# A hybrid decoder layer: joint maxima behind the last far scores, earlier splits of the output weights, value halves stored apart

## The chip, the cores and the metric

The kernel runs on one core of a Trainium2 chip. It is one program of some 17,000 instructions on five engines: TensorE (matrix products and transposes, PE in the profile; its weight loads are PEld), VectorE (DVE), ScalarE (ACT), GpSimd (POOL) and SyncE (SP), whose queue issues the DMAs. Each engine works through its own row of instructions in order, and waits at an instruction until the semaphores that it needs have come. The metric is the device time of one execution in microseconds.

## The reference

One decoder layer on 1024 tokens of width 1024:

```python
h = rmsnorm(x, mix_pre_norm)
q_a, k_a, v_a, q_h, f_h, i_h, g_h = split(h @ w_in)
attn = dilated_mixture_attention(q_a, k_a, v_a, slopes)   # 8 heads of 64
attn = rmsnorm(attn, attn_out_norm)
rec = hgrn2_recurrence(q_h, f_h, i_h, g_h, lower_bounds)  # 4 heads of 128
x = x + rmsnorm(concat([attn, rec]) @ w_out, mix_post_norm)
h = rmsnorm(x, mlp_pre_norm)
x = x + rmsnorm(square(relu(h @ w_ff1)) @ w_ff2, mlp_post_norm)
```

In the attention a token sees keys in three dilated windows, and the three softmaxes are joined by their denominators. That is one softmax over all keys with a table of biases. The recurrence ends in `o = rmsnorm(o) * silu(gate)`. All is float32.

## The kernel before

A float32 product is made of three passes: each operand is split into a high part, which TensorE takes in its fast form, and the low rest, and high by high, high by low and low by high are added. Such a split is a copy on ScalarE (`hi`) and a subtraction on VectorE (`lo = src - hi`, L85 and L86). The weights come as tiles of 128 by 1024 in the order of a list, `stream`. `w_load` (L102) fetches the next one into one of two raw buffers, `w_split` (L109) splits the next one and then asks for a further load, and `w_get(i)` (L125) splits all up to `i`. The eight tiles of the output weights follow those of the projections in this list, from WO0 on. `WO_TAG` says in which kind of buffer their parts lie: a pair of names is two slab buffers, None the two buffers `wh` and `wl` of the projections. The profile calls the parts `woh` and `wol` in the first case, `wh` and `wl` in the second.

The four recurrent heads come first (`hgrn_core`, L453), then the eight attention heads, two to a pair. The gate products (`gated`, L608) are the end of a recurrent head: eight VectorE instructions of 128 by 128 that multiply the normed output, still in PSUM, by the gate. For the last recurrent head they are put off into the attention, four in step 0 and four in step 2.

The attention is a hand-written loop of 64 steps (L1244), eight to a head. A step belongs to one piece of the scores of its head: D0 to D3 are the first four blocks of 128 rows, F0 and F1 the far keys of the later rows (by class of four), N0 and N1 their near keys. For a piece there is

- `look` (L813): two score matmuls into a bank of kind "s"; VectorE adds the bias, writes the scores to SBUF and takes the maximum of each row (a custom instruction and a read of its accumulator, L842);
- `raise_` (L881): ScalarE's exponential with the negative maximum as bias;
- `turn` (L894): TensorE transposes the exponentials into a bank of kind "t"; ScalarE copies the high part out, VectorE subtracts the low part;
- `weigh` (L936) and `finish` (L975): the product with the values, and a transpose back.

There are two banks of each kind. A matmul into one waits until what stood in it two banks ago has been read.

The far and the near scores of a row share one maximum, but their rows lie in two orders. So the maxima are carried over: `spread_max` (L862) is a VectorE product of the maxima with a selector, `swap_max` (L870) two small TensorE matmuls into a bank "s" (the profile's `px`), and `joint` (L875) two small VectorE instructions that take the larger maximum and negate it. `joint(hd, 0)` ends the maxima of the far rows and must stand before their exponentials, `joint(hd, 1)` does so for the near rows. Before the change the near maxima are spread at the end of step 0 and swapped at the end of step 1, the far ones spread at the end of step 2 and swapped at the end of step 3; `joint(hd, 0)` opens step 3 and `joint(hd, 1)` step 4 (steps counted within the head).

Between these pieces `fill` (L172) takes matmuls from a queue of generators, so many per step as `UNITS` says: first the projections of the coming pairs (`attn_proj`, L728), from step 47 on the first half of the output product (`early_out`, L1092, TensorE's `pwe`), for which rows of the recurrence's result are multiplied by a gain on GpSimd (`row_rec`, L1033, the profile's `erows`) and transposed (`row_turn`, L1066, `pmt` and `emt`). What is to be done at a certain step beside that stands in a table, `hooks` (L1214). Steps 40 to 47 are head 5, 48 to 55 head 6, 56 to 63 head 7. `drain` (L187) issues all that is left in the queue.

The values of a pair are made in two halves of 512 tokens. `values_turn` (L712) transposes a half (`pvt`, from VectorE's `vf`), splits it, and after the second half stores both to DRAM with four DMAs. `far_load` (L637) loads the values of the far keys from there in another order with six DMAs, into two tiles. `key_job` (L695) copies a piece of the keys' high part, subtracts the low part on GpSimd (`kl`), and lets SyncE copy both to the other half of the partitions.

## Time and profile before

| | us |
|---|---|
| median of 3 runs | 1214.13 (1213.41 to 1214.55) |
| the profiled execution | 1214.51 |
| its span, first to last instruction | 1212.7 |
| TensorE busy | 1198.3 (99%) |
| VectorE busy | 868.8 (72%) |
| ScalarE busy | 546.6 (45%) |
| GpSimd busy | 326.3 (27%) |
| TensorE between 450 and 500 us | 46.09 of 50 |

The granted TensorE clock was 0.999. The profile divides the span into forty slices; TensorE is at nine tenths or more in all but the first and the last. The end of a matmul is modelled, so two neighbours overlap in the listing, and a wait shows as a late start with the idle time in brackets and the instruction that ended it. The attention's 64 steps run from 306 to about 520 us; step 40 begins near 443 and step 47 near 466. A step is found in TensorE's row by its transposes: one to four for D0 to D3, three for F0 and F1, four for N0 and N1.

### The profile page before, as it was taken

To read this page: it belongs to the slowest core of one execution; us is meant where nothing else is said; L and a number is where in the kernel's file an instruction comes from. 1 tells how busy PE (TensorE), PEld (TensorE's weight loads), DVE (VectorE), ACT (ScalarE), POOL (GpSimd) and SP (SyncE) were. 2 spreads that over 40 slices of the span, in tenths; PEclk is the share of its full clock that TensorE was granted. 3 is DMA by queue.
4 is the path that set the end of the run, shared out by engine and by line. 5 is a ranking of instruction groups with operands and counts; after the bars stand their busy time and mean duration, and the time that the engine had idled before them with its cause. 6 is when DMAs were issued, how large, how long until landed. Compare 5 with 4: busy or idle time off the path is not lost.

```text
span 1212.7 us, 17220 instructions
## 1 busy us (share of the span) xinstructions
PE 1198.3 (99%) x6350; PEld 1026.8 (85%) x6350; DVE 868.8 (72%) x1478; ACT 546.6 (45%) x1067; POOL 326.3 (27%) x321
## 2 busy tenths in 40 slices
PE   8999999999999999999999999999999999999998
PEld 8898989888888887888888888888888888888886
DVE  5697878777666767677689566766678554478796
ACT  7633333322565657755565222222234453534562
POOL 0110102022221213254230886575631000000022
PEclk9999999999999999999999999999999999999999
DMA  5231323123544546364514555553587534433337
GB/s 218 69 94 58 104 75 108 36 82 75 141 109 117 141 118 146 104 218 145 188 64 156 182 174 209 192 185 140 199 324 266 212 92 152 158 102 100 109 104 278
DMA packets 86483, 174.21 MB, mean 144 GB/s; under 512 B 12160, under 2 KB 38784, under 8 KB 86400
## 3 DMA queue, kind: packets, MB, share of 16 engines
q1 hardware_dynamic: 86400, 173.12, 44.0%
q8 instruction: 50, 0.82, 0.3%
q14 instruction: 33, 0.27, 0.1%
HBM read 117.76 MB, written 49.04 MB: 138 GB/s over the span
## 4 chain that ended last, share of the span: by engine, by line
PE 93%; DVE 2%; ACT 2%; DMA 1%; issue 1%; POOL 0%; SPq 0%; DVEq 0%; POOLq 0%; ACTq 0%
PE f L1940 18%; PE f2s L1940 7%; PE pig L91 2%; PE pig L89 2%; PE pig L90 2%; PE pl L480 2%; PE pwo L91 2%; PE pwo L89 2%; PE pwo L90 2%; PE pm_ak L89 1%; PE pm_f L89 1%; PE pm_ak L91 1%; PE pm_ak L90 1%; PE pm_f L91 1%; PE pm_f L90 1%; PE pm_av L89 1%
## 5 line engine op out<-in xcount | busy, mean ns | idle before, releaser
L86 DVE TENSOR_TENSOR al<-ar,ah 128x1024 fp32r<-128x1024 f32 x56 | 70.6, 1261 | 80.7 <-ACT ah L85 80.6
L1940 PE MATMUL f<-bh,ah 128*128 128x512 f32 x320 | 124.5, 389 | 0.0
L1940 PE MATMUL f<-bl,ah 128*128 128x512 f32 x320 | 124.5, 389 | 0.0
L1940 PE MATMUL f<-bh,al 128*128 128x512 f32 x320 | 124.5, 389 | 0.0
L85 ACT ACTIVATE ah<-ar 128x1024 fp32r<-128x1024 f32 x56 | 59.1, 1056 | 87.5 <-DMA ar<-actd 87.2
L1940 PEld LDWEIGHTS f<-bh,al 128*128 128x128 f32 x320 | 60.1, 188 | 12.6
L1940 PEld LDWEIGHTS f<-bl,ah 128*128 128x128 f32 x320 | 60.1, 188 | 12.5
L1940 PEld LDWEIGHTS f<-bh,ah 128*128 128x128 f32 x320 | 60.1, 188 | 12.3
L2014 POOL TENSOR_SCALAR lbl<-ssq 128x1 f32<-128x1 f32 x4 | 3.3, 819 | 245.7 <-ACT fd L2010 245.6
L1563 POOL TENSOR_TENSOR e<-x,e 128x512 f32<-128x512 f32 x14 | 21.6, 1540 | 131.0 <-DVE x L1514 123.8
L1940 PE MATMUL f2s<-bl,ah 128*128 128x512 f32 (+1 forms) x128 | 48.9, 382 | 0.0
L1940 PE MATMUL f2s<-bh,al 128*128 128x512 f32 (+1 forms) x128 | 48.9, 382 | 0.0
L1940 PE MATMUL f2s<-bh,ah 128*128 128x512 f32 (+1 forms) x128 | 48.9, 382 | 0.0
L671 POOL COPY tout<-traw 128x256 f32<-128x256 f32 x16 | 12.2, 763 | 107.9 <-DMA traw<-in_bias_tab_dram 74.2
L991 POOL TENSOR_TENSOR anat<-anat,stat 128x128 f32<-128x128 f32 (+1 forms) x24 | 13.4, 559 | 102.4 <-DVE anat L990 91.1
L86 DVE TENSOR_TENSOR bl<-br,bh 128x1024 fp32r<-128x1024 f32 x32 | 40.1, 1253 | 1.1 <-ACT bh L85 1.0
L1957 ACT ACTIVATE acc<-f 128x512 f32<-128x512 f32 x28 | 16.7, 598 | 49.4 <-PE f L1940 49.4
L86 DVE TENSOR_TENSOR wl<-raw,wh 128x1024 fp32r<-128x1024 f32 x23 | 30.1, 1310 | 10.9 <-ACT wh L85 10.9
L85 ACT ACTIVATE bh<-br 128x1024 fp32r<-128x1024 f32 x32 | 33.6, 1050 | 3.7 <-PE f L1940 2.4
L707 POOL TENSOR_TENSOR kl<-kf,kh 64x512 fp32r<-64x512 f32 x16 | 22.2, 1390 | 39.8 <-ACT kh L706 36.8
L751 POOL TENSOR_TENSOR ql<-qf,q 64x512 fp32r<-64x512 f32 x16 | 21.4, 1340 | 42.4 <-ACT q L750 41.8
L89 PE MATMUL pwo<-woh,mt 128*128 128x512 f32 x80 | 31.6, 395 | 0.0
(1702 smaller groups left out, 4022.5 us busy)
## 6 DMA issues: line engine op xcount, KB each, us to landing
ar<-actd SPq DMA_DIRECT2D x56, 512.0 KB, 3.7
br<-in_w_ff_dram SPq DMA_DIRECT2D x16, 1024.0 KB, 6.3
w1r<-in_w_ff_dram SPq DMA_DIRECT2D x14, 1024.0 KB, 6.5
raw<-in_w_in_dram SPq DMA_DIRECT2D x26, 512.0 KB, 4.0
actd<-e SPq DMA_DIRECT2D x17, 768.0 KB, 4.3
actd<-e SPq DMA_DIRECT2D x11, 1024.0 KB, 4.1
vd<-v SPq DMA_DIRECT2D x16, 256.0 KB, 3.9
raw<-in_w_out_dram SPq DMA_DIRECT2D x8, 512.0 KB, 3.7
```

The lines of the kernel that those rows point to most:

```text
L85: S.activation(hi, src, AF.Copy)
L86: eng.tensor_tensor(out=lo, in0=src, in1=f32(hi), op=ALU.subtract)
L89: TE.matmul(dst, lhs[0], rhs[0], start=start, stop=False)
L90: TE.matmul(dst, lhs[0], rhs[1], start=False, stop=False)
L91: TE.matmul(dst, lhs[1], rhs[0], start=False, stop=stop)
L480: TE.matmul(pl[:, n % 2, :192], kt[:, n * P:(n + 1) * P], sets[u // 2][:, n % 4], start=True, stop=True)
L707: G.tensor_tensor(out=kl[a:b], in0=src, in1=f32(kh[a:b]), op=ALU.subtract)
L751: G.tensor_tensor(out=lo[a:b], in0=full[a:b], in1=f32(stacks[i]["q"][a:b, sl]), op=ALU.subtract)
L991: G.tensor_tensor(out=dst, in0=dst, in1=st["rd"][:, b].unsqueeze(2).to_broadcast([P, n, 64]), op=ALU.mult)
L1563: eng[0].tensor_tensor(out=e1[:, 3], in0=a21, in1=e1[:, 2], op=ALU.add)
L1940: TE.matmul(pm, a[:, j, c], b[:, j, d], start=start and j == 0 and q == 0, stop=stop and j == 1 and q == 2, skip_group_check=True)
L1957: S.activation(acc_at(p, i), pm, AF.Copy)
```

## The change

Five things are moved or cut otherwise; nothing that is computed changes.

1. Joint maxima and spreads. `joint(hd, 0)` and then the spread of the far maxima now stand in step 2 of a head, right behind the look at F1 (the last far scores). The far maxima are swapped at the end of step 2, and `joint(hd, 1)` stands near the end of step 3.
2. The gate products of the last recurrent head go in twos, in steps 0 to 3.
3. The first four output tiles are split in steps 43, 44, 45 and 47 (before: 44, 45, 47 and 48). The first two now lie in slabs, the third and fourth in `wh` and `wl`. The subtraction of the fourth runs on GpSimd.
4. The transposes of the last value half and the far load of the last pair move from step 48 to step 47, ahead of that split in program order; row products move from 48 and 49 to 49 and 50.
5. `values_turn` stores each half by itself: four blocks of the first half, and of the second only the two that the far keys reach. `far_load` fills its first tile before its second.

```diff
-    WO_TAG = (None, ("S", "S"), ("S", "BT"), None, ("S", "S"), ...
+    WO_TAG = (("S", "S"), ("S", "BT"), None, None, ("S", "S"), ...
...
-        def gated(g4):
-            for n in range(g4 * 4, g4 * 4 + 4):
-                V.scalar_tensor_tensor(gate[:, n], pos[g4][:, n % 4], rs[:, n:n + 1], gate[:, n],
+        def gated(g2):
+            for n in range(g2 * 2, g2 * 2 + 2):
+                V.scalar_tensor_tensor(gate[:, n], pos[n // 4][:, n % 4], rs[:, n:n + 1], gate[:, n],
...
-        for odd in range(2):
-            for c, p0, k0, n in ((0, 0, 64 * odd, P), (1, 0, P - P * odd, 64), (1, 64, P - P * odd, 64)):
+        for c in range(2):
+            for odd in range(2):
+                for c_, p0, k0, n in ((0, 0, 64 * odd, P), (1, 0, P - P * odd, 64), (1, 64, P - P * odd, 64)):
+                    if c_ == c:
...
-        if hf == 1:
-            for r in range(DIL):
-                nc.sync.dma_start(out=v_dram[pr][r].rearrange("(n i) c -> i n c", i=32),
-                                  in_=f32(vs[32 * r:32 * r + 32]).rearrange("p n h a d -> p n (h a d)"))
-            if pr == 0:
-                far_load(0)
+        b = slice(0, 4) if hf == 0 else slice(4, 6)
+        for r in range(DIL):
+            nc.sync.dma_start(out=v_dram[pr][r].rearrange("(n i) c -> i n c", i=32)[:, b],
+                              in_=f32(vs[32 * r:32 * r + 32, b]).rearrange("p n h a d -> p n (h a d)"))
+        if hf == 1 and pr == 0:
+            far_load(0)
...
         0: lambda: last_gate(0),
-        2: lambda: last_gate(1),
-        43: lambda: row_rec(0),
-        44: lambda: [row_rec(1), w_get(WO0, 0)],
-        45: lambda: w_get(WO0 + 1, 0),
+        1: lambda: last_gate(1),
+        2: lambda: last_gate(2),
+        3: lambda: last_gate(3),
+        43: lambda: [row_rec(0), w_get(WO0, 0)],
+        44: lambda: [row_rec(1), w_get(WO0 + 1, 0)],
+        45: lambda: w_get(WO0 + 2, 0),
         46: lambda: row_turn(0, 0),
-        47: lambda: [drain(), w_get(WO0 + 2, 0), early_sums(), queue.extend(early_out(t) for t in range(NE))],
-        48: lambda: [values_turn("t"), far_load(AH // 2 - 1), w_get(WO0 + 3, 0), row_rec(2)],
-        49: lambda: [load_bias(AH - 1), row_rec(3)],
-        50: lambda: row_turn(1, 0),
+        47: lambda: [drain(), values_turn("t"), w_split(G), far_load(AH // 2 - 1), early_sums(),
+                     queue.extend(early_out(t) for t in range(NE))],
+        49: lambda: [load_bias(AH - 1), row_rec(2)],
+        50: lambda: [row_turn(1, 0), row_rec(3)],
...
-        if i in (3, 4):
-            joint(hd, int(i == 4))
...
+        if i == 2:
+            joint(hd, 0)
+            spread_max(hd, 1)
         kind, g = ITEMS[i]
         turn(hd, kind, g)
...
-        if i in (0, 2):
-            spread_max(hd, int(i == 2))
+        if i == 0:
+            spread_max(hd, 0)
+        elif i == 3:
+            joint(hd, 1)
...
-        if i in (1, 3):
-            swap_max(hd, int(i == 3))
+        if i in (1, 2):
+            swap_max(hd, i - 1)
```

Three places show what this does to the rows of the engines. The first is TensorE in step 47, before: the transposes of N1 (`pt_N`), the first N products with the values, then the first output product (`pwe`) and the near scores of head 6 (`ps_N`).

```order
L911 MATMUL pt_N_5043<-ident,pn_4749 128x128 x4
L966 MATMUL pov_far<-ptNh_5005,v_3907 128x4x32
L966 MATMUL pov_far<-ptNl_5006,v_3907 128x4x32
L966 MATMUL pov_far<-ptNh_5005,v_3907 128x4x64
L966 MATMUL pov_far<-ptNl_5006,v_3907 128x4x64
L89 MATMUL pwe_0_5062<-wh_4950,emt_4778 128x512
L90 MATMUL pwe_0_5062<-wl_4951,emt_4778 128x512
L91 MATMUL pwe_0_5062<-wh_4950,emt_4778 128x512
L837 MATMUL ps_N_5068<-kh_0_4671,q_0_4431 128x256
```

And TensorE at the same place of the changed kernel:

```order
L913 MATMUL pt_N_5065<-ident,pn_4765 128x128 x4
L968 MATMUL pov_far<-ptNh_5027,v_3919 128x4x32
L968 MATMUL pov_far<-ptNl_5028,v_3919 128x4x32
L968 MATMUL pov_far<-ptNh_5027,v_3919 128x4x64
L968 MATMUL pov_far<-ptNl_5028,v_3919 128x4x64
L718 MATMUL pvt_5076<-ident,vf_5057 128x128 x4
L89 MATMUL pwe_0_5103<-woh_4932,emt_4794 128x512
L90 MATMUL pwe_0_5103<-wol_4933,emt_4794 128x512
L91 MATMUL pwe_0_5103<-woh_4932,emt_4794 128x512
L839 MATMUL ps_N_5109<-kh_0_4683,q_0_4443 128x256
```

The transposes of the last value half (`pvt`) have come in, ahead of the first output product. Before, they stand 23 rows further on, in step 48.

The second is VectorE from the near scores of step 48 into step 49, before: `swap_0` is a spread, `v` the low part of the values, `wl` that of an output tile, `pd` the read of the scores D3 and `pf` that of F0.

```order
L842 ISA pn_5067,stat_4996<-ps_N_5099,bt_4683 128x256
L842 ISA stat_4996 128x1
L865 TENSOR_TENSOR swap_0_5106<-stat_4996,pick_133 128x128
L720 TENSOR_TENSOR v_4568<-pvt_5108,v_4568 128x8x64
L86 TENSOR_TENSOR wl_5128<-raw_4990,wh_5127 128x1024
L842 ISA pd_4997,stat_4996<-ps_D_5138,bt_4683 128x512
L842 ISA stat_4996 128x1
L845 TENSOR_SCALAR stat_4996<-stat_4996 128x1
L932 TENSOR_TENSOR ptl_0_5083<-pt_D_5143,pth_0_5082 128x2x128
L934 RECIPROCAL stat_4996<-stat_4996 128x2
L842 ISA pf_4998,stat_4996<-ps_F_5152,bt_4683 128x192
```

And VectorE there with the change:

```order
L844 ISA pn_5108,stat_5018<-ps_N_5140,bt_4695 128x256
L844 ISA stat_5018 128x1
L867 TENSOR_TENSOR swap_0_5147<-stat_5018,pick_133 128x128
L844 ISA pd_5019,stat_5018<-ps_D_5153,bt_4695 128x512
L844 ISA stat_5018 128x1
L847 TENSOR_SCALAR stat_5018<-stat_5018 128x1
L934 TENSOR_TENSOR ptl_0_5124<-pt_D_5158,pth_0_5123 128x2x128
L936 RECIPROCAL stat_5018<-stat_5018 128x2
L844 ISA pf_5020,stat_5018<-ps_F_5167,bt_4695 128x192
```

The two subtractions `v` and `wl` have gone from here: `v` stands in step 47, `wl` on GpSimd.

The third is SyncE from step 44 on, before: copies of the keys, loads of raw tiles of the output weights, the swap of the far denominators through DRAM (`swd`), the stores of the values (`vd`) and the loads of the far values (`vf`).

```order
L710 DMA kl_0_4672<-kl_0_4672 64x4x128
L106 DMA raw_4954<-in_w_out_dram 128x1024
L854 DMA swd_649<-stat_4685 128x4
L106 DMA raw_4990<-in_w_out_dram 128x1024
L857 DMA stat_4685<-swd_649 128x4x1
L710 DMA kh_1_4673<-kh_1_4673 64x4x128
L710 DMA kl_1_4674<-kl_1_4674 64x4x128
L106 DMA raw_5058<-in_w_out_dram 128x1024
L723 DMA vd_635<-v_4568 32x8x256 x4
L642 DMA vf_0_5119<-vd_635 128x2x256
L642 DMA vf_1_5120<-vd_635 64x2x256 x2
```

And SyncE with the change:

```order
L106 DMA raw_4936<-in_w_out_dram 128x1024
L106 DMA raw_4976<-in_w_out_dram 128x1024
L856 DMA swd_649<-stat_4697 128x4
L106 DMA raw_5012<-in_w_out_dram 128x1024
L859 DMA stat_4697<-swd_649 128x4x1
L712 DMA kh_1_4685<-kh_1_4685 64x4x128
L712 DMA kl_1_4686<-kl_1_4686 64x4x128
L725 DMA vd_635<-v_4582 32x2x256 x4
L106 DMA raw_5091<-in_w_out_dram 128x1024
L644 DMA vf_0_5093<-vd_635 128x2x256 x2
L644 DMA vf_1_5094<-vd_635 64x2x256 x4
```

Three raw loads instead of two stand ahead of the last key copies, the last stores have two blocks instead of eight, and one raw load (`raw_5091`, which takes the buffer that GpSimd's subtraction reads) stands between them and the loads of the far values.

## What was predicted

> **What bounds the kernel now.** I read the page first, for the engine without slack.
>
> ```profile
> span 1212.7 us, 17220 instructions
> PE 1198.3 (99%) x6350; PEld 1026.8 (85%) x6350; DVE 868.8 (72%) x1478; ACT 546.6 (45%) x1067; POOL 326.3 (27%) x321
> ```
>
> TensorE is busy for 1198.3 of 1212.7 us, and the change leaves its matmuls as they are (the swap matmuls and the transposes of the values stand elsewhere in its row, none is new). A gain can only come out of its waits. So the second view is the list of what TensorE waited for in the whole span: total, times, longest.
>
> ```profile
> PE ps_F L837 <- DVE stat L842: 1.3, 2, 0.7
> PE pt_N L911 <- DVE ptNl L932: 0.9, 2, 0.7
> PE pov_far L960 <- DMA vf<-vd: 0.7, 1, 0.7
> PE ps_N L837 <- DVE stat L842: 0.5, 1, 0.5
> ...
> PE pwe L89 <- ACT esum L1101: 0.5, 1, 0.5
> PE ps_D L837 <- DVE stat L842: 0.4, 1, 0.4
> PE pt_F L914 <- DVE ptFh L929: 0.3, 1, 0.3
> PE pt_F L914 <- ACT pf L892: 0.2, 1, 0.2
> ```
>
> These are all the waits of the attention, 4.8 us in ten places. The third view is TensorE's timeline there (start, length, instruction, idle in brackets); it puts one of them into head 0 and the other nine between 465 and 508 us, from step 47 on.
>
> ```profile
> 312.27 0.36 PE L837 MATMUL ps_F<-kh,qc 128*128 128x192 f32 x1 [0.58 <-DVE stat L842]
> ...
> 464.80 0.28 PE L837 MATMUL ps_D<-kh,q 128*128 128x256 f32 x1
> 464.91 0.28 PE L838 MATMUL ps_D<-kl,q 128*128 128x256 f32 x1
> 465.86 0.66 PE L911 MATMUL pt_N<-ident,pn 128*128 128x128 f32 x4 [0.67 <-DVE ptNl L932]
> ...
> 466.81 0.40 PE L89 MATMUL pwe<-wh,emt 128*128 128x512 f32 x1
> ...
> 479.28 0.47 PE L89 MATMUL pwe<-wh,emt 128*128 128x512 f32 x1
> ...
> 507.96 0.50 PE L89 MATMUL pwe<-wh,emt 128*128 128x512 f32 x1 [0.50 <-ACT esum L1101]
> ```
>
> A bracket counts from the modelled end of the matmul before. The bracket of 0.67 is not the whole loss: the matmuls from 464.80 to 464.91 follow each other after 0.11 us, and the next starts 0.95 after that, so its wait cost 0.84, about 0.15 more than the bracket. I add 0.15 to each, which makes some 6 us in all that the change could reach. Steps 3 to 46 show no wait at all, so what it does there can only lose.
>
> **The change part by part.**
>
> Gate products in twos. The wait at 312.27 is the last far score of head 0: its bank is free when VectorE has read the far scores before it.
>
> ```profile
> 309.36 1.11 DVE L610 SCALAR_TENSOR_TENSOR gate<-po,hrs,gate 128x128 f32<-128x128 f32 x4
> 310.40 0.67 DVE L842 CUSTOM_DVE_ANT_0 pd<-ps_D,bt 128x512 f32<-128x512 f32 x1
> ...
> 311.85 0.35 DVE L842 CUSTOM_DVE_ANT_0 pf<-ps_F,bt 128x192 f32<-128x192 f32 x1
> ```
>
> The four products take 309.36 to 310.40, 1.04 us, and all reads behind them are that late. With two of them moved behind these reads, the second read ends 0.52 earlier. Of 0.58 + 0.15 = 0.73 that wins **0.5** (bounds 0.3 and 0.7). The other products stand where VectorE waits anyway, in steps 1 to 3, at nothing; without that cover each pair would cost 0.52.
>
> Splits in steps 43 to 47, and the transposes of the values in step 47. Here I expect a new wait. The order shows the transposes of the last value half right behind the four N products of step 47, and they read `vf`, which VectorE writes late:
>
> ```profile
> 466.42 0.69 DVE L86 TENSOR_TENSOR emt<-pmt,emt 128x512 fp32r<-128x512 f32 x1 [0.62 <-ACT emt L85]
> 467.03 1.08 DVE L764 TENSOR_TENSOR vf<-pm_av,rrow 128x512 f32<-128x512 f32 x1
> ...
> 455.67 0.46 ACT L892 ACTIVATE pf<-pf,stat 128x192 f32<-128x192 f32 x1 [1.69 <-DVE stat L879]
> ...
> 462.48 1.04 ACT L85 ACTIVATE woh<-raw 128x1024 fp32r<-128x1024 f32 x1
> ...
> 465.79 0.60 ACT L85 ACTIVATE emt<-pmt 128x512 fp32r<-128x512 f32 x1
> ```
>
> The chain is ScalarE's: from the split copy that begins at 462.48 (call that X) it runs on to `emt` at X + 3.3, and `vf` is written by X + 5.6. In the new row the copy at this place is the third split's instead of the second's, and one copy (about 1 us) stands ahead of it in addition. It is paid by the earlier far maxima, since ScalarE loses the 1.69 us in which it stood for them. But the third split also needs its raw tile, which can be loaded only when the first split has released the buffer:
>
> ```profile
> 459.63 0.59 SPq L710 DMA_DIRECT2D kl<-kl  x1
> 462.03 0.35 SPq L106 DMA_DIRECT2D raw<-in_w_out_dram  x1
> ...
> 458.32 1.28 POOL L707 TENSOR_TENSOR kl<-kf,kh 64x512 fp32r<-64x512 f32 x1
> 459.57 3.57 POOL L1035 TENSOR_TENSOR erows<-erows,etable 128x512 f32<-128x512 f32 x2
> ...
> raw<-in_w_out_dram SPq DMA_DIRECT2D x1, 512.0 KB, 3.6
> ...
> raw<-in_w_out_dram SPq DMA_DIRECT2D x1, 512.0 KB, 5.0
> ```
>
> On SyncE it follows the copy of the keys that starts at 459.63, which itself follows GpSimd's 1.28 us at 458.32. With the maxima earlier I put GpSimd's piece about a microsecond earlier and the load at 458.8 to 459.4; with 3.6 us to land that is X = 462.4 to 463.0 (with 5.0, X = 464.1). So `vf` is ready at 468.0 to 468.6, and TensorE, which is through with step 47's N products at 466.81, waits 1.2 to 1.8 us. In return VectorE has caught up behind it: the waits of 0.4 and 0.5 for the scores of head 6 go, 1.2 with their 0.15 each. Net 0 to -0.6, and as X may be no later than before I take **-0.2** (bounds +0.4, and -1.6 with the load of 5.0).
>
> Step 48 loses its split and its transposes. VectorE had there:
>
> ```profile
> 473.91 1.22 DVE L86 TENSOR_TENSOR wl<-raw,wh 128x1024 fp32r<-128x1024 f32 x1 [0.25 <-ACT wh L85]
> ```
>
> This 1.22 us, now on GpSimd, delayed the reads of the far scores, and with them the wait of step 50 (the 1.3 of the list less 0.58, so 0.7). It goes whole: **0.9** with its 0.15. What covers the slower subtraction on GpSimd: its result is wanted by the fourth product of the output tile, first at 479.28 in the row of before; the copy that it follows should end near 470, and two pieces of 1.3 us (the rate of `kl` above) end at 473.
>
> Joint maxima and spreads one step earlier. The waits of 0.2 and 0.3 for the far exponentials and their parts in steps 52 and 53 follow a chain on ScalarE that stood for the maxima. With the maxima ready before step 51 begins, ScalarE is held by its own row alone, some 0.3 us earlier. Of 0.8 (with 0.15 each) I take **0.5** (bounds 0 and 0.8).
>
> Value halves stored separately, and all of it a step earlier:
>
> ```profile
> 473.69 3.04 SPq L723 DMA_DIRECT2D vd<-v  x4
> 479.44 3.64 SPq L642 DMA_DIRECT2D vf<-vd  x6
> ...
> 484.24 0.58 SPq L798 DMA_DIRECT2D etable<-tabd  x1
> ...
> vd<-v SPq DMA_DIRECT2D x4, 256.0 KB, 4.2
> ...
> etable<-tabd SPq DMA_DIRECT2D x1, 352.0 KB, 7.2
> ...
> 491.65 0.29 DVE L842 CUSTOM_DVE_ANT_0 pd<-ps_D,etable 128x128 f32<-128x128 f32 x1 [2.70 <-PE pmt L1078]
> ```
>
> The last stores now begin when VectorE has written the half, about 470, move a quarter of the bytes, and with 4.2 us to land let the six loads begin at about 475.5 instead of 479.44. The one raw load that SyncE meets ahead of them waits for GpSimd's subtraction, about 473, so it delays nothing. The loads come four microseconds earlier, TensorE two: the wait of 0.7 goes, **0.9** (lower bound 0). Sixteen more DMAs on SyncE over four pairs lie where its queue has room. Behind these loads stands the bias table of head 7: issued at 484.24 and 7.2 us on its way it landed at 491.4, and VectorE's first read of it began at 491.65 after 2.70 idle. That delay is what the second wait of `pt_N` (0.9 - 0.67, 0.2) came from; four microseconds earlier it is gone, **0.4** (lower bound 0).
>
> The wait for `esum` near 508 stays: its chain passes none of the moved work. Sum: 0.5 - 0.2 + 0.9 + 0.5 + 0.9 + 0.4 = 3.0 us. The profiled execution took 1214.51 us, 1.8 more than its span, and lies 0.38 above the median of 1214.13: it would become 1211.5, and the median **1211.1**, which I predict. Both are 0.25% lower.
>
> **The rivals.**
>
> The raw tile comes late. If the third split's load takes 5.0 us, X moves by 1.4, everything to the transposes of the values with it, and the time is 1212.5. Against it: nothing else of size is on the way at 459 us. If it took as long as the bias table, 7.2 us, the loss is 3.6 and the result 1214.7, slower than before; the sign turns at a landing of 3.6 + 3.0 = 6.6 us.
>
> The swap matmul of step 50 takes over. It now stands at the end of this step and needs the spread on VectorE, while row products run on GpSimd:
>
> ```profile
> 478.39 1.29 POOL L1035 TENSOR_TENSOR erows<-erows,etable 128x512 f32<-128x512 f32 x1
> ...
> 479.05 0.88 DVE L865 TENSOR_TENSOR swap<-stat,pick 128x128 f32<-128x128 f32 x1
> ```
>
> The spread took 0.88 us next to such a product and ended only when that had ended, and the two products at 459.57 took 3.57 together, against 1.29 for one, across VectorE's split at 460.8. The change puts two products into steps 49 and 50, right beside the joint maximum and the spread. If both go first, the swap matmul comes 0.7 us late, step 50 wins 0.2 instead of 0.9, and the time is 1211.8. The Trainium skill's page "SBUF — State Buffer", section "Who interferes with whom", gives the rule: a VectorE instruction with two inputs in SBUF and a GpSimd instruction that reads SBUF exclude each other, and the later one stands for the whole length of the other. The rows agree, and by this rule moving a subtraction to GpSimd is not free either, where VectorE has a two-input instruction beside it; in step 48 it has only a short spread.
>
> The loads of the far values don't come earlier, because the raw load ahead of them on SyncE stands for GpSimd's subtraction, stretched by VectorE's work as at 459.57. Then the last two gains go, and the time is 1212.4. Against it: the stretching there was 1.0 us, and the reserve is two.
>
> **How the numbers follow.** Forecast 0.50; load late 0.15, very late 0.05; swap matmul 0.15; far values not earlier 0.10; a new wait that I don't see, in heads 0 to 4 too, 0.05. About 0.2%, 2.4 us, is what a measurement of this kernel can tell from no change, so faster means below 1211.7. The forecast alone misses it by 0.6, so of its half I count 0.44; of the swap matmul's 0.10, and 0.04 of the others: 0.58 faster. Slower (above 1216.6) needs a load of 9 us, longer than any row shows, or the wait that I don't see: 0.08. The rest, 0.34, is the same. The high bounds together win 0.7 + 0.4 + 0.9 + 0.8 + 0.9 + 0.4 = 4.1 us, 1210.0; a wait near 508 that shrinks as well could give 1209.6. Upwards the range takes in the late load and the missing far values, and some of both: 1213.3.
>
> **What would show it.** TensorE's wait list: no wait for `vf<-vd`, none for the far score of step 50, the wait of head 0 down to some 0.2 in its bracket; a new row of 1 us or more, `pvt` waiting for VectorE's `vf`. The second `pt_N` wait gone, the first still there. The third split's copy on ScalarE between 462 and 463 us after the same start. If `px` shows up among the waits, the second rival holds; if `pt_N` and `pvt` both grow, the first. Any wait of TensorE between 320 and 460 us would make me wrong where I didn't look for it.

## The result, and the profile after

| | before | after |
|---|---|---|
| median, us (executions) | 1214.12 (22) | 1212.02 (22) |
| lowest to highest | 1212.91 to 1215.13 | 1210.83 to 1213.62 |
| the profiled execution | 1214.51 | 1211.49 |
| its span | 1212.7 | 1209.7 |
| predicted median | | 1211.1 (1209.6 to 1213.3) |

The ratio is 0.9984, with a 95% interval of 0.9977 to 0.999. The change wins 0.16%, 2.1 us: the direction that was forecast, two thirds of the size, and less than the 0.2% that I had set as the limit for "faster". The profiled execution is 3.0 us shorter, exactly the forecast sum, but that agreement is partly luck, as the parts will show: 0.36 of it arose in the first 12 us of the program, which the change does not touch, and the median fell by less.

The page of the kernel after shows TensorE as before, with the same number of matmuls:

```profile
span 1209.7 us, 17250 instructions
...
PE 1197.2 (99%) x6350; PEld 1026.8 (85%) x6350; DVE 869.5 (72%) x1477; ACT 546.0 (45%) x1067; POOL 327.5 (27%) x322
```

Its list of TensorE's waits (total, times, longest) is shorter in the attention:

```profile
PE pig L291 <- DVE nhalf L229: 1.4, 1, 1.4
PE pt_N L913 <- DVE ptNl L934: 1.3, 1, 1.3
PE xt L267 <- DMA xr<-in_x_dram: 1.2, 1, 1.2
PE pvt L718 <- DVE vf L766: 1.2, 1, 1.2
PE pwe L89 <- ACT esum L1103: 0.6, 1, 0.6
PE pig L314 <- ACT wig0h L85: 0.3, 1, 0.3
PE pt_F L916 <- DVE ptFh L931: 0.2, 1, 0.2
```

All waits for scores (`ps_F`, `ps_N`, `ps_D`), the one for the far values and the second of the two `pt_N` waits are gone. In their place stands the new wait of the values' transposes (`pvt`, 1.2), and the first `pt_N` wait has doubled (0.67 before). TensorE's timeline of the kernel after, at the places of the prediction:

```profile
311.45 0.36 PE L839 MATMUL ps_F<-kh,qc 128*128 128x192 f32 x1
...
465.57 0.66 PE L913 MATMUL pt_N<-ident,pn 128*128 128x128 f32 x4 [1.34 <-DVE ptNl L934]
...
467.87 0.66 PE L718 MATMUL pvt<-ident,vf 128*128 128x128 f32 x4 [1.18 <-DVE vf L766]
468.29 0.47 PE L89 MATMUL pwe<-woh,emt 128*128 128x512 f32 x1
...
483.72 0.52 PE L916 MATMUL pt_F<-ident,pf 128*128 128x128 f32 x3 [0.25 <-DVE ptFh L931]
```

Laid beside TensorE's row of before, instruction by instruction, the lead of the kernel after grows by 0.36 at the program's start, 0.48 at head 0's far score (312.27 before, 311.45 now), and 0.13 in step 44. It shrinks by 0.70 in steps 46 and 47. Then it grows by 1.02 at step 50, 0.5 in steps 51 to 53, 0.96 at the far values, and 0.45 behind the bias table of head 7. From 493 us on it stays at 3.04. (These parts come to 3.20; shifts of about 0.1 where the swap matmuls have changed places make up the difference.)

What delays step 47 is read from the timelines of GpSimd, VectorE, SyncE's queue and ScalarE, kernel after:

```profile
456.29 1.29 POOL L709 TENSOR_TENSOR kl<-kf,kh 64x512 fp32r<-64x512 f32 x1
457.53 4.55 POOL L1037 TENSOR_TENSOR erows<-erows,etable 128x512 f32<-128x512 f32 x2
...
456.60 2.10 DVE L86 TENSOR_TENSOR wol<-raw,woh 128x1024 fp32r<-128x1024 f32 x1 [0.55 <-ACT woh L85]
...
458.72 2.59 SPq L106 DMA_DIRECT2D raw<-in_w_out_dram  x2
...
462.20 1.06 ACT L85 ACTIVATE wh<-raw 128x1024 fp32r<-128x1024 f32 x1 [0.69 <-DMA raw<-in_w_out_dram]
...
463.29 1.23 DVE L86 TENSOR_TENSOR wl<-raw,wh 128x1024 fp32r<-128x1024 f32 x1 [0.80 <-ACT wh L85]
...
464.83 0.68 DVE L934 TENSOR_TENSOR ptNl<-pt_N,ptNh 128x512 fp32r<-128x512 f32 x1
466.16 0.69 DVE L86 TENSOR_TENSOR emt<-pmt,emt 128x512 fp32r<-128x512 f32 x1 [0.65 <-ACT emt L85]
466.77 1.04 DVE L766 TENSOR_TENSOR vf<-pm_av,rrow 128x512 f32<-128x512 f32 x1
```

The first split's subtraction, now in step 43, starts 0.3 us after GpSimd's subtraction of the keys and takes 2.10 instead of 1.23. It releases the raw buffer that much later; the third raw tile is issued at 458.72 and lands at 462.20, for which ScalarE waits 0.69. Behind this copy stand `ptNl` (TensorE's wait of 1.34) and, further on, `vf` (its wait of 1.18).

The far values and the bias table come much earlier. SyncE's queue and VectorE's first read of the table, kernel after:

```profile
469.92 1.77 SPq L725 DMA_DIRECT2D vd<-v  x4
...
473.13 3.62 SPq L644 DMA_DIRECT2D vf<-vd  x6
477.43 0.58 SPq L800 DMA_DIRECT2D etable<-tabd  x1
...
486.80 0.29 DVE L844 CUSTOM_DVE_ANT_0 pd<-ps_D,etable 128x128 f32<-128x128 f32 x1
```

The six loads start 6.3 us earlier than before (479.44), the table 6.8 (484.24), and neither has a bracket behind it any more.

### The profile page after: what moved, and what is told of

It is laid out like the page before. It is cut to its first block, busy times and chain, and to the rows that moved or that the text cites. A ratio compares the mean times of both kernels' runs of the same rounds, so it can differ in the third digit from the quotient of the medians.

```text
span 1209.7 us, 17250 instructions
## 1 busy us (share of the span) xinstructions
PE 1197.2 (99%) x6350; PEld 1026.8 (85%) x6350; DVE 869.5 (72%) x1477; ACT 546.0 (45%) x1067; POOL 327.5 (27%) x322
## 4 chain that ended last, share of the span: by engine, by line
PE 94%; ACT 2%; DVE 2%; DMA 1%; issue 1%; SPq 0%; POOL 0%; DVEq 0%; POOLq 0%; ACTq 0%
PE f L1947 18%; PE f2s L1947 7%; PE pig L91 2%; PE pig L89 2%; PE pig L90 2%; PE pl L480 2%; PE pwo L91 2%; PE pwo L89 2%; PE pwo L90 2%; PE pm_ak L89 1%; PE pm_f L89 1%; PE pm_ak L91 1%; PE pm_ak L90 1%; PE pm_f L91 1%; PE pm_f L90 1%; PE pm_av L89 1%
```

## The experiments

Each kernel is a variant of the kernel after, and each ratio is to the kernel before on the same chip (medians of before 1214.29 to 1214.47). "Offset" below is the start of the same TensorE instruction against the profiled execution of the kernel after.

**Gate products in fours again.**

```diff
-        0: lambda: last_gate(0),
-        1: lambda: last_gate(1),
-        2: lambda: last_gate(2),
-        3: lambda: last_gate(3),
+        0: lambda: [last_gate(0), last_gate(1)],
+        2: lambda: [last_gate(2), last_gate(3)],
```

> The changed kernel with the gate products in fours again (two pairs in step 0, two in step 2), all else kept. If the gain at head 0 is that of the twos, as the prediction had it (0.5), TensorE's wait for the far score of head 0 grows back to about 0.6 and all of its row behind 312 us is 0.4 to 0.5 later than in the changed kernel: about 1212.5. The rival is that the twos had nothing to do with it (another bank became free, or the start of the program differed from one execution to the next): then the row behind 312 us stands as in the changed kernel, within 0.1, and the time is 1212.0.

Median 1213.54, ratio to before 0.9992 (0.9983 to 1.0001). The far score of head 0 waits again, and TensorE's row is 0.49 later from there on: the gain of the twos, as predicted. But at the end it is 2.07 later. Its timeline, and two windows around the end of step 47 (stretch, length, busy time and count of PE, PEld, DVE, ACT and POOL, then the granted clock, DMA share and GB/s):

```profile
311.94 0.35 PE L839 MATMUL ps_F<-kh,qc 128*128 128x192 f32 x1 [0.59 <-DVE stat L844]
...
469.23 0.78 PE L89 MATMUL pwe<-woh,emt 128*128 128x512 f32 x1
...
464.92:468.33 3.41, 1.12 (x8) 0.92 (x8) 2.72 (x8) 2.73 (x8) 1.28 (x1) 1.00 0.52 144
468.33:471.74 3.41, 3.27 (x12) 2.99 (x13) 1.87 (x6) 2.03 (x4) 0.44 (x1) 0.50 0.47 87
```

In this execution the clock was halved from 468.3 to 471.7, at the end of the waits of step 47: the product took 0.78 us where it took 0.47 in the kernel after, and TensorE lost 1.6 us. I had not thought of that. The profiled execution of the kernel after shows clock 1.00 in the same place; its other executions follow below.

**Joint maxima, spreads and swaps in their old places.**

```diff
+        if i in (3, 4):
+            joint(hd, int(i == 4))
...
-        if i == 2:
-            joint(hd, 0)
-            spread_max(hd, 1)
...
-        if i in (1, 2):
-            swap_max(hd, i - 1)
+        if i in (1, 3):
+            swap_max(hd, int(i == 3))
```

> The changed kernel with the joint maxima, the spreads and the swap matmuls in their old places. By the prediction (0.5 in steps 51 to 53) the waits of 0.2 and 0.3 for far exponentials and their parts come back there. Besides, ScalarE stands again some 1.7 us for the maxima in step 43, ahead of the split copies: if the copy of the third split then begins by its own row and no longer by the raw tile's landing, the waits in step 47 grow by 0.3 to 1. Together 0.5 to 1.5 slower than the changed kernel: 1212.5 to 1213.5. The rival is that the order of the maxima is worth nothing and that the gain there came from VectorE being freed in step 48: then no wait comes back in steps 51 to 53, and the time is 1212.0.

Median 1213.57, ratio 0.9991 (0.9983 to 1.0). All of TensorE's waits between 456 and 484 us:

```profile
459.69 0.44 PE L916 MATMUL pt_F<-ident,pf 128*128 128x128 f32 x2 [0.32 <-ACT pf L894]
461.59 0.33 PE L962 MATMUL pov_far<-ptFl,vf 128*128 128x128 f32 x1 [0.71 <-DVE ptFl L929]
467.35 0.66 PE L913 MATMUL pt_N<-ident,pn 128*128 128x128 f32 x4 [0.98 <-DVE ptNl L934]
469.33 0.66 PE L718 MATMUL pvt<-ident,vf 128*128 128x128 f32 x4 [0.87 <-DVE vf L766]
482.86 0.44 PE L916 MATMUL pt_F<-ident,pf 128*128 128x128 f32 x2 [0.17 <-ACT pf L894]
```

The offset grows by 0.6 at step 51 (the 0.5 of the prediction), and by 1.2 in steps 43 to 47. So the joints are worth more than I gave them: with the splits already in step 43, the late maxima would have held up the far transposes and products there, by two waits of 0.32 and 0.71. No execution had a mean clock under 0.998.

**The split of step 47 on VectorE.**

```diff
-        47: lambda: [drain(), values_turn("t"), w_split(G), ...
+        47: lambda: [drain(), values_turn("t"), w_split(), ...
```

> The changed kernel with the subtraction of step 47's split on VectorE instead of GpSimd. If it is VectorE's 1.2 us that made TensorE wait for the scores of steps 48 to 50, as the prediction had it (0.9), waits for scores of 0.5 to 1.3 in sum come back between 470 and 477 us, and the time is about 1212.9. The rival is that it was the step earlier that removed the wait, whichever engine does it: VectorE stands idle for 0.6 us at 471.5 and takes the rest there, and TensorE loses at most 0.3, which makes 1212.0 to 1212.3.

Median 1213.06, ratio 0.9988 (0.9979 to 0.9997). In the profiled execution no wait for a score came back. The offset is 0.22 up to step 47 and 1.77 from 472 us on, and all of this difference is a halved clock between the two (468.4 to 471.8). But that leaves the question open, since the half clock covers the very place. VectorE and TensorE:

```profile
470.59 1.23 DVE L86 TENSOR_TENSOR wl<-raw,wh 128x1024 fp32r<-128x1024 f32 x1 [0.26 <-ACT wh L85]
471.73 0.42 DVE L844 CUSTOM_DVE_ANT_0 pn<-ps_N,bt 128x256 f32<-128x256 f32 x1
...
473.12 0.33 PE L839 MATMUL ps_N<-kh,q 128*128 128x256 f32 x1
```

The reads of the near scores begin behind the split, 1.7 us later than in the kernel after (469.81, and 0.22 of offset), and the second ends at 472.49. TensorE wants their bank at 473.12; without the 1.55 that it lost to the clock it would have come at 471.57 and, by this estimate, waited some 0.9, the size that the prediction had for this split. The four executions with a mean clock of 0.999 or more took 1212.12 to 1213.66, against 1210.83 to 1212.15 for those of the kernel after on a chip where the kernel before is 0.35 shorter. That points to the waits, and so to the engine, but no trace of an execution at full clock shows it.

**The values in step 48 again, or stored together again.**

```diff
-        47: lambda: [drain(), values_turn("t"), w_split(G), far_load(AH // 2 - 1), early_sums(),
+        47: lambda: [drain(), w_split(G), early_sums(),
                      queue.extend(early_out(t) for t in range(NE))],
+        48: lambda: [values_turn("t"), far_load(AH // 2 - 1)],
```

> The changed kernel with the transposes of the last value half, its stores and the far loads of the last pair in step 48 again. If the new wait in step 47 is worth its 1.2 us, it goes, and TensorE is about 1.2 ahead of the changed kernel at 472 us. The price: stores and loads come 2 to 4 us later, so the wait for the far values (0.7 to 0.9) and the second wait of the N transposes (0.2 to 0.4) come back by 493 us, and the copies of the values stand ahead of the far scores again (0 to 0.5). Net 0.6 faster to 0.6 slower than the changed kernel, 1211.4 to 1212.6. The rival is that step 47's waits are one chain from the raw tile: with the transposes gone from there, the next matmuls wait instead, nothing is won at 472 us, and it ends at 1213.0 or above.

Median 1211.15 (1210.84 to 1211.49, six executions), ratio 0.997 (0.9959 to 0.9982): lower than the kernel after, though the two intervals overlap a little and the chips differ. TensorE and SyncE's queue:

```profile
466.17 0.66 PE L913 MATMUL pt_N<-ident,pn 128*128 128x128 f32 x4 [1.45 <-DVE ptNl L934]
...
468.85 0.44 PE L839 MATMUL ps_D<-kh,q 128*128 128x384 f32 x1 [0.36 <-DVE stat L844]
...
475.12 4.84 SPq L644 DMA_DIRECT2D vf<-vd  x6
```

The second wait of step 47 is gone, a wait of 0.36 for the scores of head 6 is back, and neither the far values nor the bias table are waited for, though the loads run 2 us later. Its profiled execution started 0.45 late (a load of `x` at the program's start), so the 0.18 by which it ends ahead make 0.63.

The other half of this part, the stores:

```diff
-        for r in range(DIL):
-            nc.sync.dma_start(out=v_dram[pr][r]...[:, b], in_=f32(vs[32 * r:32 * r + 32, b])...)
+        if hf == 1:
+            for r in range(DIL):
+                nc.sync.dma_start(out=v_dram[pr][r]..., in_=f32(vs[32 * r:32 * r + 32])...)
```

> The changed kernel with the value halves stored together again, behind the second half (the far loads in their new order, and all of it in step 47 as in the changed kernel). It tells which part won the wait for the far values (0.7 to 0.9) and the wait behind the bias table (0.2 to 0.4). If the earlier step wins them, neither wait comes back, since loads that begin about 1.3 us later than in the changed kernel still land well ahead: 1212.0. If the separate stores win them, the wait for the far values is back at 484 us with 0.5 or more: 1212.5 to 1213.

Median 1212.69, ratio 0.9988 (0.9979 to 0.9997); in the profiled execution neither wait came back, and TensorE's row lies within 0.05 of the kernel after from the first wait of step 47 to the end. So with either half of this part alone the 0.96 and the 0.45 are won; the second one adds nothing. The new order of the far loads stands in both kernels, and no run undoes it, so what it does by itself is open.

**The two waits of step 47.** Three kernels: the first split ahead of the keys in step 43; the low part of the first transposed row (`emt`) behind the write of `vf`; both.

```diff
+        if s == 43:
+            w_get(WO0, 0)
         if i in (1, 2, 3, 6, 7):
             key_job()
...
-        43: lambda: [row_rec(0), w_get(WO0, 0)],
+        43: lambda: row_rec(0),
```

> The changed kernel with the first split of step 43 issued ahead of the copies and the subtraction of the keys in that step, instead of behind them. Theory: the first split's subtraction on VectorE took 2.1 us where it stood beside GpSimd's subtraction of the keys (1.29 us); without it beside, it takes 1.23 and begins 0.6 earlier, the third raw tile is loaded about 1 us earlier, ScalarE's 0.7 us of waiting for it goes, and the wait of the N transposes in step 47 falls from 1.3 to some 0.6; the wait for vf stays at 1.2, since all of that chain moves together. TensorE 0.7 earlier at 470 us than in the changed kernel, and the half clock in fewer executions or in none. About 1211.0. Rival: ScalarE's own row is no shorter, or the key copies now come late and something waits for them: the wait of the N transposes stays above 1.1, and the time is 1212.0 or above.

```diff
-        46: lambda: row_turn(0, 0),
+        46: lambda: row_turn(0, 0, later=True),       # transposes and ScalarE's copy
-        47: lambda: [drain(), values_turn("t"), ...
+        47: lambda: [drain(), held_low(), values_turn("t"), ...   # VectorE's low part
```

> The changed kernel with one VectorE instruction moved: the low part of the first transposed row (emt, 0.69 us, with 0.65 us of waiting for ScalarE ahead of it) stands behind the write of vf instead of ahead of it, step 47. Theory: vf is then written 1.3 us earlier, TensorE's wait of 1.2 us for it goes, the wait of the N transposes ahead of it (1.3) stays, and TensorE is 1.0 to 1.2 earlier than the changed kernel at 470 us, with nothing given back. And since only one of the two waits is left, the TensorE clock does not fall to half behind them in any execution, as it did in some executions of the changed kernel (half clock for some 3 us, 1.3 us lost): mean clock 0.999 in all runs, all times within 0.8 us of each other, about 1210.8 in the median. Rival to the first: the row products that use emt wait instead (0.3 to 0.7), and 0.5 is won. Rival to the second: the half clock has nothing to do with these waits, and the executions still fall into two groups 1.3 apart.

> Both of these moves together (first split ahead of the keys in step 43; the low part of the first transposed row behind vf in step 47). If the two waits of step 47 are two chains, as the theory has it, the gains add up: the N transposes wait some 0.6, the transposes of the values not at all, TensorE is 1.7 to 1.9 earlier at 470 us than in the changed kernel, no half clock: 1210.0 to 1210.4. If it is one chain, it gains no more than the better one of the two alone.

The medians are 1211.37, 1213.18 and 1212.05, the ratios 0.9984 (0.9975 to 0.9994), 0.999 (0.9981 to 0.9998) and 0.9981 (0.9972 to 0.999). With the split ahead of the keys, VectorE, GpSimd and TensorE:

```profile
456.57 1.33 DVE L86 TENSOR_TENSOR wol<-raw,woh 128x1024 fp32r<-128x1024 f32 x1
...
457.13 1.92 POOL L709 TENSOR_TENSOR kl<-kf,kh 64x512 fp32r<-64x512 f32 x1 [0.31 <-ACT kh L708]
...
465.32 0.65 PE L913 MATMUL pt_N<-ident,pn 128*128 128x128 f32 x4 [0.61 <-DVE ptNl L934]
```

The subtraction that comes first keeps its length and the other is stretched; the wait of the N transposes falls from 1.34 to 0.61, the offset by 0.71. That is the price of the meeting in step 43. The wait for `vf` stayed at 1.2. Moving `emt` won nothing, VectorE and TensorE:

```profile
465.05 1.09 DVE L766 TENSOR_TENSOR vf<-pm_av,rrow 128x512 f32<-128x512 f32 x1
...
466.78 0.69 DVE L934 TENSOR_TENSOR ptNl<-pt_N,ptNh 128x512 fp32r<-128x512 f32 x1
467.39 0.68 DVE L1092 TENSOR_TENSOR emt<-pmt,emt 128x512 fp32r<-128x512 f32 x1
...
467.53 1.11 PE L718 MATMUL pvt<-ident,vf 128*128 128x128 f32 x4 [1.22 <-DVE ptNl L934]
```

`vf` is written 1.7 us earlier by the listing (0.3 of that is an earlier start of the program), and the transposes of the values wait as long as before, now for `ptNl`, at whose end (467.47) they start. They go into a bank of kind "t", of which there are two. One still holds the transposed row, which `emt` now reads later, and the other holds this step's own N transposes until `ptNl` is subtracted. So the wait has two conditions, `vf` and a free bank, of which a profile names only the later one. In the kernel after the bank was free by 466.85, when `emt` had read it; the move that made `vf` earlier made the bank later. The kernel with both moves gains no more than the first alone (its waits are 0.87 and 1.10). Two executions of the kernel with the split ahead of the keys took 1215.70 and 1216.18, longer than one half clock explains; no trace shows why.

**Work in the waits.** Is it the idle time that halves the clock? The N transposes of step 47 are issued three times, with the same values into the same bank: 0.84 us of TensorE work more, ahead of the second wait.

```diff
+            times = 3 if (hd, kind, g) == (5, "N", 1) else 1
-            for u in range(4 if kind == "N" else 3):
+            for u in [*range(4)] * times if kind == "N" else range(3):
```

> The changed kernel with the four N transposes of step 47 issued three times instead of once (the same values into the same bank): 0.84 us of TensorE work more, put between its two waits of 1.3 and 1.2 us. Nothing else moves. Theory: the idle share of some 3.4 us of TensorE's row lets the clock fall to half for 3.4 us. With the work in it the second wait shrinks to about 0.4, the transposes of the values start when they did, the half clock goes from all executions, and the time falls although TensorE has more to do: mean clock 0.999 in every execution, times within 1 us of each other, median 1211.4 to 1211.8. Rival: the half clock comes from something else at that place (what is computed, or the length of the first wait): the executions fall into two groups as before, and the median is 1212.0 to 1212.9.

Median 1211.64, ratio 0.998 (0.9971 to 0.9988).

```profile
466.14 1.53 PE L914 MATMUL pt_N<-ident,pn 128*128 128x128 f32 x12 [1.39 <-DVE ptNl L935]
...
468.47 0.66 PE L718 MATMUL pvt<-ident,vf 128*128 128x128 f32 x4 [0.34 <-DVE vf L766]
```

The transposes of the values start where they did (the offset is that of the program's start, 0.54 to 0.60), and the times lie within 0.85 us of each other. The gain is in the spread: on the same chip the kernel after itself has no higher a median, but a mean of 1212.1 against 1211.7 here:

> The changed kernel itself once more, on the same chip as the three runs beside it. By its first runs: 1211.9 to 1212.1 in the median, some executions at a mean clock of 0.999 below 1212.1, the others at 0.997 to 0.998 and 1.0 to 1.5 us longer.

Median 1211.48, 1210.94 to 1214.43, ratio 0.9984 (0.9975 to 0.9993). The executions with their mean clocks, all kernels (the waits are those of the one profiled execution of each; a mean clock of 0.998 stands in both kinds of kernel and is not counted):

| kernel | waits in step 47, us | executions | mean clock 0.997 or less | lowest to highest, us |
|---|---|---|---|---|
| after (both sets) | 1.34, 1.18 | 33 | 8 | 1210.83 to 1214.43 |
| gate in fours | 1.42, 1.19 | 11 | 6 | 1212.47 to 1215.31 |
| stores together | 1.48, 1.2 | 11 | 4 | 1211.46 to 1214.73 |
| split on VectorE | 1.3, 1.2 | 11 | 4 | 1212.12 to 1214.68 |
| emt late | 1.36, 1.22 | 11 | 3 | 1211.90 to 1214.81 |
| first split ahead of the keys | 0.61, 1.2 | 11 | 3 | 1210.56 to 1216.18 |
| both moves | 0.87, 1.10 | 11 | 4 | 1210.46 to 1214.53 |
| joints in old places | 0.98, 0.87 | 11 | 0 | 1212.87 to 1214.05 |
| work in the waits | 1.39, 0.34 | 11 | 0 | 1211.34 to 1212.19 |
| values in step 48 | 1.45, none | 6 | 0 | 1210.84 to 1211.49 |
| values in step 48, split ahead of the keys | 1.58, none | 8 | 0 | 1209.90 to 1211.85 |
| the same, third subtraction on GpSimd | 1.63, none | 6 | 0 | 1209.61 to 1211.59 |
| before | 0.67, none | 86 | 0 | 1212.73 to 1216.30 |

In the kernel after's first 22 executions the twelve with a mean clock of 0.999 have a median of 1211.53; the ten with 0.997 or 0.998 lie between 1212.21 and 1213.62. The medians of the two groups lie 1.4 apart. I put that down to the half clock, though no profiled execution of this kernel shows it: in the four traces of other kernels with 3.4 us of it, TensorE lost 1.3 to 1.6 us by it. By the mean clock it comes in some executions of every kernel that has a second wait of 1.1 us or more closely behind a first (32 of 99), and in none of the changed kernels in which the second wait is shorter than that, missing, or filled with work (0 of 42). The two kinds of execution belong to the kernel's result; its median lies between them.

**Combinations.** The values in step 48 and the first split ahead of the keys; then, in addition, the subtraction of the third split on GpSimd.

```diff
-        45: lambda: w_get(WO0 + 2, 0),
+        45: lambda: w_split(G),
```

> The changed kernel with the last value half, its stores and its loads in step 48 and the first split of step 43 ahead of the keys. Each was tried alone: the first took away the second wait of step 47 (net 0.6 won), the other made the first wait 0.6 to 0.9 instead of 1.3 to 1.4. If they add up, one wait of 0.6 to 0.9 is left, and no execution shows the half clock: 1210.4 to 1210.8. Rival: VectorE, now a little ahead, meets the next wait (scores of head 6, 0.4 so far), and nothing is added: 1211.2.

> As the run before it, and the third split's subtraction (step 45) on GpSimd too. VectorE loses 1.23 us of work between 463 and 466 us, where it is what the N transposes wait for. Theory: their wait falls to 0.2 or less and the wait for the scores of head 6 goes: 1209.6 to 1210.2. Rival: the subtraction takes 2.4 us or more on GpSimd, and the next copies of the keys and the fourth split stand behind it: a product of the output tile waits for its weights, and nothing is won: 1210.8 or above.

The medians are 1210.72 (1209.90 to 1211.85, ratio 0.9971, 0.9961 to 0.9982) and 1210.05 (1209.61 to 1211.59, ratio 0.997, 0.9958 to 0.9981). Both beat the kernel before and, on the same chip, the kernel after (1211.48), by 0.8 and 1.4 us in the medians, with no execution at a low clock. The mechanism that I expected of them didn't show. Of the first, SyncE's queue and ScalarE; of the second, ScalarE and TensorE:

```profile
457.76 0.36 SPq L106 DMA_DIRECT2D raw<-in_w_out_dram  x1
...
462.76 1.06 ACT L85 ACTIVATE wh<-raw 128x1024 fp32r<-128x1024 f32 x1 [0.94 <-DMA raw<-in_w_out_dram]
```

```profile
463.04 1.06 ACT L85 ACTIVATE wh<-raw 128x1024 fp32r<-128x1024 f32 x1 [1.40 <-DMA raw<-in_w_out_dram]
...
466.00 0.66 PE L913 MATMUL pt_N<-ident,pn 128*128 128x128 f32 x4 [1.63 <-DVE ptNl L934]
```

The raw tile was asked for 1.0 us earlier than in the kernel after and took 5.0 us instead of 3.5; the copies of the keys are now issued right behind it, which may be the reason. ScalarE waits for it in both profiled executions, each one of the slower of its kernel. In the one profiled execution of the split ahead of the keys alone, with the same order of issues, the tile was there in time, after 4.0 us at most. How often the load is late I can't tell from single traces; nor is it shown where the last 0.7 us of the best kernel come from.

## Why the prediction was right, and where it was wrong

- **Gate in twos, 0.5:** 0.48 in the trace, and 0.49 when undone. Right.
- **Step 48 without its split, 0.9:** 1.02. The size and place are right. Whether VectorE had to be rid of the subtraction for it, as I had it, or only step 48, is not settled: the one trace with the split on VectorE has the half clock at this place.
- **Joint maxima earlier, 0.5:** 0.5 in the trace, 0.6 when undone. But undone they cost another 1.2 in steps 43 to 47. I had put their effect on ScalarE there into the term of the splits and not seen that without them the splits would hold up the far keys.
- **Far values, 0.9, and bias table, 0.4:** 0.96 and 0.45. The sizes are right. I had counted on the separate stores and the earlier step together; either does it.
- **Splits in steps 43 to 47, -0.2:** this is the term that was mis-sized: -0.70 in the profiled execution, and some 2.1 lost in those with the half clock. The chain was right, and its start was not. I placed the third split's copy, X, at 462.4 to 463.0 on the clock of before, and took -0.2 because X might come no later than before. It started at 462.20, and with the lead of 0.85 that TensorE then had that is 463.05, just past the edge. By the prediction's own steps `vf` is then ready at 468.65 and TensorE loses 1.84, of which 1.2 come back: -0.64. The two waits of step 47 bear the 1.84 out, 0.67 more for the N transposes and 1.18 for `vf`. That I left the first of them at its old 0.67 was a second mistake, since its `ptNl` stands behind the same split on VectorE; it moved the loss from one wait to the other and added nothing to it. The half clock is no term of the sum at all.

The lateness of X has a cause that I had in hand. I weighed the exclusion of VectorE and GpSimd at two other places and not where the change itself puts VectorE's two-input subtraction next to GpSimd's keys, step 43; there it cost 0.7. The Trainium skill's page "SBUF — State Buffer", section "Who interferes with whom", gives this as an exclusive lock of a shared port pair, and the rows agree: whichever of the two came later was stretched, 1.23 to 2.10 us or 1.29 to 1.92.

Of the rivals, the late raw tile is what happened in part: it landed in 3.5 us, as forecast, but was asked for later. The swap matmul of step 50 never waited, and the far values came early. Of the 0.9 between the forecast median and the measured one, 0.4 is there in the twelve executions without the half clock (1211.53); the other ten put the median at 1212.02.

## What to carry to other kernels

When an instruction is moved later, go through everything that stands behind it on its engine and give each consumer the delay, not only the one that was the reason to look. Where two waits of a microsecond come close together on a TensorE that is otherwise busy, expect to pay for the clock as well, and look at the granted clock of several executions before a difference of a few tenths of a per cent is put down to an edit. Undoing the parts one by one is worth it even for a change that wins: here the one part that was moved a step too far, the values' transposes, cost 0.6 us in the trace and brought the half clock. And read the granted clock around the place before a missing wait is taken for an answer: a slow TensorE hides what VectorE does late.

## What the runs showed of the hardware

The clock of TensorE fell to half for 3.4 us (twice that in the profiled execution with `emt` late: 466.7 to 473.5) during or right behind two waits of together 1.8 to 2.6 us with 1.1 us of matmuls between them, in some executions and not in others. The Trainium skill's page "TensorE: Matmul & The Clock Gate", section "Part 1: The HAM clock gate (the "warmup" mystery)", speaks of a window of about 3.4 us that runs freely and after whose idle passing the clock is halved. The length that we see agrees, and a free-running window would make it a matter of chance which executions are hit. But no window here was idle.

The traces' record of the clock says more. In all five traces with a fall, it comes 460.8 us after the clock rose to full at the start, which is 135 times 3.413 us, though that rise lies anywhere from 5.9 to 7.6 us. So I cut each of the 14 traces, from its own rise on, into pieces of 3.413 us, and took the piece between 455 and 480 us in which TensorE worked least. In the five it held 1.12, 1.42, 1.61, 1.68 and 1.73 us of work, and the clock fell at its end. In the nine others it held 1.78 to 2.67, and the clock stayed. The closest two are the kernel with both moves, which fell, and the one with the third subtraction on GpSimd, which did not; of each the piece and the one behind it:

```profile
463.31:466.72 3.41, 1.73 (x12) 1.28 (x10) 3.34 (x10) 2.85 (x8) 1.28 (x1) 1.00 0.44 58
466.72:470.13 3.41, 3.12 (x12) 2.83 (x13) 1.52 (x3) 1.97 (x4) 0.29 (x1) 0.50 0.73 199
```

```profile
462.70:466.11 3.41, 1.78 (x13) 1.45 (x13) 1.11 (x4) 3.02 (x7) 2.33 (x2) 1.00 0.38 127
466.11:469.53 3.42, 3.04 (x17) 2.24 (x18) 2.49 (x6) 2.97 (x7) 2.18 (x3) 1.00 0.59 148
```

So in these traces what counts is the work within one piece, with a limit between 1.73 and 1.78 us of 3.41, about half; the modelled ends of matmuls can shift these figures a little. It would also explain why executions of one kernel differ, though no kernel has a trace of each kind. With the gate in fours both waits lay in one piece (1.12); in the profiled execution of the kernel after, whose clock rose at 4.75, a boundary fell between them (2.09 and 2.21). A single wait of 1.45 to 1.63 us left 1.78 or more, and in 20 executions of the three kernels with such a wait the mean clock never fell to 0.997.
